# Splitting the long rows of a load into descriptors of at most 7 KB in a DMA-bound im2col kernel

## Chip, cores, metric

The kernel runs on one core of a Trainium2 chip. Times are device microseconds (us) of whole executions, as the device reports them. Durations of single packets are in nanoseconds (ns). An execution that is over 1.5% above the fastest of its kernel counts as slow, the others as fast; ratios compare fast ones alone. A ratio whose 95% interval lies within 2% of 1 gets the verdict "same".

## The reference

The reference unfolds 3x3 patches of a batch of images (im2col). Input: 16 images, 64 channels, 32x32, float32, 4.19 MB. Output: 16 x 576 x 900, 33.18 MB.

```python
for b in range(batch):
    for i in range(h_out):            # 30
        for j in range(w_out):        # 30
            patch = x[b, :, i:i + 3, j:j + 3].copy()
            cols[b, :, col_idx] = patch.ravel()
            col_idx += 1
```

## The kernel before

Each of 128 partitions takes 8 channels (256 image rows of 128 bytes, 32 KB). Three loads bring them in: rows 0 to 32 (4,096 bytes per partition), rows 32 to 200 (21,504 bytes, "the bulk"), rows 200 to 256 (7,168 bytes). VectorE (DVE) and ScalarE (ACT) copy 72 shifted windows into output tiles. Five stores write them out: two of one channel each (32,400 bytes per partition), three of two channels (64,800 bytes). All eight DMAs are issued from SP and share one queue. The first store is made to wait until the bulk load has landed; below that wait is called the gate.

```python
    def load(queue, r0, r1):
        return queue.dma_start(
            out=in_flat[:, r0 * W : r1 * W], in_=x_v[:, r0 * W : r1 * W]
        )

    cuts = [0, H, 200, CPP * H]
    first = load(nc.sync, cuts[0], cuts[1])
    bulk = load(nc.sync, cuts[1], cuts[2])
    load(nc.sync, cuts[2], cuts[3])
    # ... cut: per pair of channels, 18 copies on DVE or ACT ...
            if c == 0:
                st = nc.sync.dma_start(out=out_v[:, s], in_=...)   # cut
                if s == 0:
                    tc.add_manual_dep(st.ins, bulk.ins.name, ...,  # cut
                        reason="the store follows the bulk of the loads")
        if c > 0:
            nc.sync.dma_start(out=out_v[:, c : c + 2]..., in_=out_tile...)  # cut
```

## Time and profile before

| What | Value |
|---|---|
| Time before the prediction, 3 runs | 91.44 us (91.39 to 91.49) |
| Time of the execution that was profiled | 91.84 us |
| DMA packets, bytes | 1152, 37.37 MB |
| DMA packets' share of 16 engines' span | 97.0% |
| DVE and ACT busy | 26% and 29% |

The page's lines are shown in the prediction. Its second section cuts the span in 40 slices. The row "DMA" there is the busy share of the 16 DMA engines in tenths. A DMA engine is not one of the compute engines: each of the 16 takes 8 partitions of every transfer here and works through its packets in order.

### The profile page before, as it was taken

What the parts mean: (1) busy time and instruction counts of PE and PEld (TensorE: products, weight loads), DVE (VectorE), ACT (ScalarE), POOL (GpSimd) and SP (SyncE); (2) the same over time, 40 slices, a digit from 0 to 9 for tenths busy, and PEclk for the clock granted to TensorE, in tenths of its full rate; (3) what the DMA queues carried; (4) which work ended last, traced back from release to release, by engine and by line L of the source; (5) the groups of instructions that cost most, each with busy time, mean ns of one, the idle gap of its engine ahead of it and who ended that gap; (6) DMA issues with size and microseconds to landing.
All of it is one profiled execution on the core that took longest, in us unless ns stands there. A gap on an engine that the chain in (4) does not pass through costs nothing.

```text
span 90.1 us, 140 instructions
## 1 busy us (share of the span) xinstructions
DVE 23.5 (26%) x43; ACT 26.2 (29%) x30; POOL 0.2 (0%) x4
## 2 busy tenths in 40 slices
DVE  0380399970000089600000399300000000000000
ACT  5391399940000089920000399300000000000000
POOL 0000000000000000000000000000000000000000
DMA  5999899999599999993799999999999999947990
GB/s 129 486 382 449 360 518 446 460 460 446 259 460 460 691 460 432 460 432 173 345 460 460 460 460 460 460 460 460 460 460 460 460 432 460 403 201 345 460 460 0
DMA packets 1152, 37.37 MB, mean 415 GB/s; under 512 B 128, under 2 KB 128, under 8 KB 384
## 3 DMA queue, kind: packets, MB, share of 16 engines
q1 hardware_dynamic: 1152, 37.37, 97.0%
HBM read 4.19 MB, written 33.18 MB: 415 GB/s over the span
## 4 chain that ended last, share of the span: by engine, by line
DMA 45%; DVE 16%; DVEq 1%; issue 0%; SPq 0%
DMA out_dram<-out_tile 35%; DVE out_tile L57 16%; DMA in_tile<-in_x_dram 11%; DVEq L93 1%; DVEq L57 0%; SPq L75 0%
## 5 line engine op out<-in xcount | busy, mean ns | idle before, releaser
L55 ACT COPY out_tile<-in_tile 128x900 f32<-128x900 f32 x29 | 24.9, 938 | 30.1 <-DMA out_dram<-out_tile 25.3
L57 DVE COPY out_tile<-in_tile 128x900 f32<-128x900 f32 x43 | 23.5, 624 | 33.6 <-DMA out_dram<-out_tile 26.0
L55 ACT ACT_TABLE_LOAD x1 | 1.3, 1283 | 0.8 <-PEq L122 0.8
L122 POOL MEMSET const-bfloat16-1.0<- 128x1 bf16 x1 | 0.1, 102 | 0.0
L122 POOL MEMSET const-uint8-127<- 128x1 uint8 x1 | 0.1, 102 | 0.0
L122 POOL MEMSET const-float32-0.0<- 128x1 f32 x1 | 0.1, 99 | 0.2 <-issue 0.2
L122 POOL MEMSET const-float32-1.0<- 128x1 f32 x1 | 0.1, 99 | 0.0
## 6 DMA issues: line engine op xcount, KB each, us to landing
out_dram<-out_tile SPq DMA_DIRECT2D x3, 8100.0 KB, 31.3
out_dram<-out_tile SPq DMA_DIRECT2D x2, 4050.0 KB, 14.9
in_tile<-in_x_dram SPq DMA_DIRECT2D x1, 2688.0 KB, 9.6
in_tile<-in_x_dram SPq DMA_DIRECT2D x1, 896.0 KB, 11.4
in_tile<-in_x_dram SPq DMA_DIRECT2D x1, 512.0 KB, 3.6
```

Of the source, the lines that this page charges most:

```text
L55: nc.scalar.copy(out=dst, in_=src)
L57: nc.vector.tensor_copy(out=dst, in_=src)
L93: tc.compile()
L122: nc = _bacc.Bacc("TRN2", target_bir_lowering=False, num_devices=1)
```

## The change

The loads pass a limit of 7,168 bytes for the last dimension of a descriptor. The intent is presumably a smoother stream of reads: pieces of equal size instead of rows of 21 KB.

```diff
     def load(queue, r0, r1):
 
         return queue.dma_start(
-            out=in_flat[:, r0 * W : r1 * W], in_=x_v[:, r0 * W : r1 * W]
+            out=in_flat[:, r0 * W : r1 * W],
+            in_=x_v[:, r0 * W : r1 * W],
+            max_dma_last_dim=7168,
         )
```

Only the bulk exceeds the limit. Each of its rows becomes three descriptors.

## The prediction

> **What bounds the kernel now.** I read the page first: the busy shares of the engines, then its slices and its DMA queue, then the DMA issues, then the queue's own waits, and last the single packet records of the trace. The page of the kernel before:
>
> ```profile
> span 90.1 us, 140 instructions
> ...
> DVE 23.5 (26%) x43; ACT 26.2 (29%) x30; POOL 0.2 (0%) x4
> ...
> DMA  5999899999599999993799999999999999947990
> ...
> DMA packets 1152, 37.37 MB, mean 415 GB/s; under 512 B 128, under 2 KB 128, under 8 KB 384
> ## 3 DMA queue, kind: packets, MB, share of 16 engines
> q1 hardware_dynamic: 1152, 37.37, 97.0%
> ...
> out_dram<-out_tile SPq DMA_DIRECT2D x3, 8100.0 KB, 31.3
> out_dram<-out_tile SPq DMA_DIRECT2D x2, 4050.0 KB, 14.9
> in_tile<-in_x_dram SPq DMA_DIRECT2D x1, 2688.0 KB, 9.6
> in_tile<-in_x_dram SPq DMA_DIRECT2D x1, 896.0 KB, 11.4
> in_tile<-in_x_dram SPq DMA_DIRECT2D x1, 512.0 KB, 3.6
> ```
>
> Both compute engines are idle for over 70% of the span, while the packets of the one DMA queue fill 97.0% of 16 engines' span. The single weaker digits of the DMA row are where slices hold few starts of long packets, not gaps (the packet records below show none). So the bound is the transfer of 37.37 MB, of which 4.19 MB are loads. The five stores are 8100 KB x3 and 4050 KB x2; the change doesn't touch them. Of the three loads, the one of 2688 KB (128 rows of 21,504 bytes) is the "21 KB per partition", the one of 896 KB (rows of 7,168 bytes) the "7 KB".
>
> Then the chain of waits, in order of time, and the queue's waits in the first 25 us:
>
> ```profile
> 0.79 9.62 DMA in_tile<-in_x_dram
> 10.41 0.02 issue
> 10.43 9.24 DVE out_tile L57 x17
> ...
> 19.74 31.24 DMA out_dram<-out_tile
> ```
>
> ```profile
> SPq L60 <- DMA in_tile<-in_x_dram: 8.8, 1, 8.8
> SPq L75 <- DVE out_tile L57: 5.5, 1, 5.5
> ```
>
> The chain seems to say that the bulk load, then 9.24 us of copies, set the end. That is misleading: the store issued at 19.74 lands 31.24 us later because it queues behind the two stores before it. Its first packet starts at 31.11 us, 11.4 us after its issue, so the copies have 11.4 us of slack (the last two stores likewise: the last is issued at 57.2 and starts at 69.40). What does matter is the first line of the queue's waits: the first store may only be issued when the bulk load has landed on all 16 engines, at 10.41 us.
>
> The packet records (start, duration and bytes of each descriptor) can be sorted to 16 engines, because on an engine each packet starts 3 to 4 ns before the end recorded for the previous one. So sorted:
> - From its first packet (1.36 to 1.71 us) to its last (88.5 to 89.13 us) each engine is never idle, except for up to 0.26 us in all in the load stage of a few. There is no gap between the last 7,168-byte packet (ends from 11.89 us on) and the first store packet.
> - Steady step from one packet to the next: 4,096 B in 155.5 ns, 7,168 B in 268 ns, 21,504 B in 795 ns, 64,800 B in 2,387 ns.
> - 15 engines end between 88.52 and 88.79 us. One ends at 89.13 us and sets the end (the span closes about 0.93 us after it; the time of 91.44 us is another 1.4 us longer). That engine lost its time at the start of the bulk load: its first 21,504-byte packets took 1,381 and 1,076 ns in place of 799, after a gap of 136 ns. Its bulk load ran from 3.155 to 10.417 us, 7.26 us against 6.36 to 6.82 us on the others. It is also the one that lands the bulk load at 10.41 us.
>
> **What the Trainium skill says.** "DMA: Bandwidth & Descriptors", section "Where 436 GB/s comes from": 435.2 GB/s is the limit of 16 ports, 27.2 bytes/ns an engine. The trace agrees: 64,800/2,387 is 27.15 bytes/ns, 21,504/795 is 27.05. Its section "Why small descriptors are slow (HBM only)" names a fixed cost of about 3 cycles per packet. Fitting the trace's steps with 27.2 bytes/ns: 268 - 263.5 = 4.5 ns, 795 - 790.6 = 4.4 ns, 155.5 - 150.6 = 4.9 ns. So about 4.5 ns per descriptor, which is of the order that page gives. Section "Why a DMA increments its semaphore by 16 and not by 1": the engine count comes from the slowest dimension, here 128 before and after, so all 16 engines still share the bulk load by partitions, and it counts as landed when the slowest of them is done; the landing at 10.41 us beside 9.74 us for the fastest engine agrees.
>
> **The change part by part.** The comparison of the instruction streams shows one difference: the bulk load's pattern is 128x3x1792 in place of 128x5376. The limit is 7,168, in bytes: 1792 floats. The first load (4,096-byte rows) and the third (exactly 7,168) stay as they are. Order, waits, semaphores, copies and stores are unchanged.
> - Removed: 128 packets of 21,504 B. Added: 384 of 7,168 B. So 256 packets more (1152 to 1408), 16 more on each engine. "Under 8 KB" should go from 384 to 768.
> - Cost in the steady state: a row goes from 795 to 3 x 268 = 804 ns, 9 ns more. Eight rows per engine: 72 ns. Since every engine is busy to the end, those 72 ns lie on the path in full.
> - Issue: a load takes SP 333 to 424 ns to issue. A third dimension may add something to one of them. The bulk is issued at 0.79 us, and its packets are first wanted at 3.0 us, so that is hidden.
> - The gate of the first store moves with the bulk by the same 72 ns, and so do the ends of the 7,168-byte packets: no new gap.
> - Intended gain, as I read it: engines with smaller pieces recover better at the start or stay more even. The most to gain is the lag of the one slow engine, 89.13 - 88.79 = 0.34 us, if it vanished.
> Sum: +0.07 us certain, and between 0 and -0.34 us for the lag. I weigh a partial gain of about 0.11 us: -0.04 us, so 91.40 us.
>
> **Rivals.**
> 1. The lag persists (for: the same addresses are read in the same order, and three executions spread only 91.39 to 91.49, so the lag seems to repeat). Then 91.44 + 0.07 = 91.51 us.
> 2. The lag vanishes, since shorter descriptors hold the engine for a shorter time when the read side is slow. For: the engine's first two bulk packets alone cost 0.58 + 0.28 us over 799. Against: the 4,096-byte packets before them stall as well (up to 984 ns in place of 159), so small packets are no cure. Then 91.44 + 0.07 - 0.34 = 91.17 us.
> 3. The stalls spread: more packets at the start, more engines hit, or another hit harder. Then the slowest ends 0.2 to 0.4 us later, 91.7 to 91.9 us.
> 4. The gate: if the bulk lands later on one engine but the others are through with their 7,168-byte packets, these idle until the store arrives. The first store is issued at 10.50 us and its first packet starts at 11.89 us, 1.39 us later; the very first load took 1.36 us from issue to packet. So the gate is only about 0.03 us from being felt. But the laggard itself has 2.15 us of third load after its bulk, more than 1.36 us, so it never waits; the others would only use up their slack of about 0.34 us against it. Up to that it costs nothing, and beyond it little: under 0.3 us.
> 5. The bulk really comes faster because 21,504-byte packets are inefficient. Against: they run at 27.05 bytes/ns against 27.15 for the largest. There is nothing to win there. If it were so for the whole stage, 1% of 6.4 us is 0.06 us.
>
> **Range and chances.** The outcomes lie between rival 2 (91.17) and rival 3 (91.9), with runs spreading 0.05 us each way and another chip perhaps 0.1. Eight in ten: 91.05 to 91.80 us. Two per cent are 1.83 us: faster by that would need a fifth of the load stage (10.6 us) to vanish while it already runs near the packets' rate; slower by that would need each of 16 new packets per engine to cost 115 ns, where the third load's packets cost 4.5. Hence 1% each, 98% within.
>
> **What would show it right or wrong.** The page should list 1408 packets. In the packet records the bulk pieces should step by 268 ns, and an undisturbed engine's bulk should take about 6.43 us in place of 6.36. The bulk's landing should lie between 9.95 us (lag gone) and 10.5 us (lag kept), and the spread of the engines' ends should show how much of the 0.34 us is left. Stores should be identical, 2,387 ns a packet, with DVE and ACT copies at 624 and 938 ns. Wrong would be: pieces stepping by clearly more than 268 ns, idle time between an engine's third load and its first store packet, or fewer than 16 engines in the bulk.

## The result

| | Median | Range | Runs |
|---|---|---|---|
| Before | 91.50 us | 91.39 to 91.53 | 6 |
| Changed | 91.66 us | 91.61 to 92.06 | 6 |

The ratio is 1.0027, with a 95% interval of 1.0009 to 1.0045; that is 0.08 to 0.41 us. A ratio is the mean time of one kernel's fast runs over the mean of the other's of the same rounds, so it is not quite the ratio of these medians. The change costs a little: 0.16 us by the medians here, and 0.12 us when all executions are pooled (91.55 us over 45 executions of the kernel before, 91.67 us over 12 of the changed one). The pool mixes chips; resampling its executions gives 0.06 to 0.22 us.

The page of the changed kernel (profiled execution: 91.61 us):

```profile
span 89.8 us, 140 instructions
...
DMA  4999999998899999875999999999999997689990
...
DMA packets 1408, 37.37 MB, mean 416 GB/s; under 512 B 128, under 2 KB 128, under 8 KB 768
## 3 DMA queue, kind: packets, MB, share of 16 engines
q1 hardware_dynamic: 1408, 37.37, 97.2%
...
in_tile<-in_x_dram SPq DMA_DIRECT2D x1, 2688.0 KB, 9.3
in_tile<-in_x_dram SPq DMA_DIRECT2D x1, 896.0 KB, 11.0
```

Two things stand out. There are 256 more packets, all under 8 KB, and the stream is still full (97.2%). And the span is *shorter* than in the first profile of before (90.1 us) although the measured times are longer. The chain of waits of the changed kernel has the bulk landing 0.30 us earlier, at 10.11 us in place of 10.41:

```profile
0.80 9.31 DMA in_tile<-in_x_dram
10.11 0.02 issue
10.13 9.24 DVE out_tile L59 x17
```

Read naively, that is a gain of 0.3 us. It is none: the first profile of before was taken on an execution of 91.84 us, that of the changed kernel on one of 91.61 us. So the first thing to test was whether the two profiles may be compared at all.

### The profile page after: what moved, and what is told of

Read it like the earlier page. It is cut to its first block, busy times and chain, and to the rows that moved or that the text cites. A ratio compares the mean times of both kernels' runs of the same rounds, so it can differ in the third digit from the quotient of the medians.

```text
span 89.8 us, 140 instructions
## 1 busy us (share of the span) xinstructions
DVE 23.5 (26%) x43; ACT 26.2 (29%) x30; POOL 0.2 (0%) x4
## 2 busy tenths in 40 slices
DMA packets 1408, 37.37 MB, mean 416 GB/s; under 512 B 128, under 2 KB 128, under 8 KB 768
## 3 DMA queue, kind: packets, MB, share of 16 engines
q1 hardware_dynamic: 1408, 37.37, 97.2%
## 4 chain that ended last, share of the span: by engine, by line
DMA 45%; DVE 16%; DVEq 1%; issue 0%; SPq 0%
DMA out_dram<-out_tile 35%; DVE out_tile L59 16%; DMA in_tile<-in_x_dram 10%; DVEq L95 1%; DVEq L59 0%; SPq L77 0%
```

## How the experiments were read

Every packet of the trace was assigned to a DMA engine as in the prediction. One correction: the prediction put all packet times 0.36 us too late against the instruction clock, because it aligned the end of the last packet of a load with the moment at which its landing was seen. The start of the first load's issue is the right zero. In the first profile of before the first packet starts at 1.01 us (not 1.36), the last engine ends at 88.77 us (not 89.13), and a landing is seen 0.35 us after the last packet's end. All packet times below are on the corrected clock. Differences between packets are not touched.

On that clock one rule holds in all 14 profiles: the time of the profiled execution is the end of the *last* DMA engine plus 3.04 to 3.11 us. "Lag" is how far that last end lies behind the mean of the 16. The prediction measured it from the second-latest engine instead; so measured, the four lags of the table are 0.34, 0.13, 0.05 and 0.19 us.

| Kernel | Profiled execution, us | Mean end of engines, us | Last end, us | Lag, us | Mean of 32,400-byte store packets, ns |
|---|---|---|---|---|---|
| before, first profile | 91.84 | 88.31 | 88.77 | 0.46 | 1,202.3 |
| before, second | 91.57 | 88.20 | 88.46 | 0.26 | 1,201.4 |
| changed, first | 91.61 | 88.30 | 88.52 | 0.22 | 1,205.0 |
| changed, second | 91.93 | 88.37 | 88.85 | 0.48 | 1,204.6 |

The split itself is seen best on engines without a stretched packet. Their eight bulk rows took 6,366 ns in both profiles of before and 6,441 ns in both of the changed kernel: 75 ns more, where the prediction said 72.

## Experiments

Kernels are compared only within the same rounds. The theories: (A) the lag is an accident of single executions, against (B) it belongs to the kernel before and the change removes it. And for the cost: (1) about 4.5 ns for each added descriptor on each engine, (2) a fixed cost of the three-dimensional pattern, (3) about 10 ns for each.

### Both kernels once more

No edit.

> The kernel before, unchanged, for a second profile. The first profile was of an execution of 91.84 us, 0.35 us above the usual 91.39 to 91.53. Theory A (the one slow DMA engine of that profile was an accident of that execution, not the kernel's habit): the new profile, if its own time is below 91.6, shows no engine that ends over 0.3 us after the rest, the bulk load lands at about 10.0 us, span about 89.7. Theory B (the lag belongs to the kernel, and the change removed it): a new profile again shows one engine ending about 0.35 us late, span 90.1. Timing: ratio 1.000 within 0.002.

Measured: 91.62 us median against 91.64 of the kernel before in the same rounds, ratio 0.9986 (0.9939 to 1.0033). The profile, of an execution of 91.57 us:

```profile
span 89.8 us, 140 instructions
...
q1 hardware_dynamic: 1152, 37.37, 97.1%
```

```profile
0.79 9.14 DMA in_tile<-in_x_dram
9.94 0.02 issue
```

The unchanged kernel lands its bulk at 9.94 us here, earlier than the changed one did. Theory A holds, theory B falls. In the bulk and the third load, 12 packets are more than 2.7% longer than usual (the longest 926 ns in place of 799), a third of the 36 in the first profile (longest 1,381).

> The changed kernel, unchanged, in the same call. Theory 1 (about 4.5 ns for each of 16 more descriptors per engine): 0.07 us over the kernel before. If the first measurement's difference of 0.16 us is real and has a second part, 0.13 to 0.19 us again. If it was chip-to-chip or run-to-run noise, it may even be near 0.

Measured: 91.68 us median (91.59 to 91.93) against 91.64, ratio 0.9988 (0.9946 to 1.0031). Runs of before were noisy (91.47 to 92.80, three of eleven above 92.1), so the ratio tells nothing about a tenth of a microsecond. The profile fell on the execution of 91.93 us:

```profile
span 90.1 us, 140 instructions
...
q1 hardware_dynamic: 1408, 37.37, 96.9%
```

```profile
0.78 9.69 DMA in_tile<-in_x_dram
10.47 0.02 issue
```

Now the changed kernel has the laggard: a lag of 0.48 us (0.19 behind the second-latest), and the bulk lands at 10.47 us. So both kernels have executions with a late engine and executions without. Over 91.85 us were 7 of the 45 executions of before and 2 of the 12 of the changed kernel.

### The bulk in 12 pieces

```diff
-            max_dma_last_dim=7168,
+            max_dma_last_dim=7168 if r0 != H else 1792,
```

> Only the bulk load changed further: each row of 21,504 bytes in 12 descriptors of 1,792 instead of 3 of 7,168. That is 88 more per engine than before. Theory 1 (4.5 ns each, on the bound path in full): 0.40 us over the kernel before, packets stepping by about 70 ns. Theory 2 (the cost is fixed, from the third dimension of the pattern or its issue): about 0.16 us, as with 3 pieces. Theory 3 (each descriptor costs about 10 ns, as 0.16 us over 16 would give): 0.88 us.

Measured: 92.46 us (92.35 to 92.50), 0.82 us over the median of before; ratio 1.0067 (1.0026 to 1.0109). By the medians this met theory 3, and not theory 1; the interval of the ratio (0.24 to 1.0 us) leaves room for both, because the runs of before were noisy. The packet records say more. In the first six of the 16 sixteenths of the bulk's packets nearly all took 74 ns (a step of 70 to 71, 4 to 5 ns over 1,792/27.2 = 65.9, theory 1 again). From about 5.7 us on the packets took 79.8 ns on average, scattered between 74 and 86. So there is a descriptor cost of 4 ns, and a second term of about 6 ns that comes and goes. What sets it on was not found.

### The bulk in 24 pieces

```diff
-            max_dma_last_dim=7168,
+            max_dma_last_dim=7168 if r0 != H else 896,
```

> The bulk load's rows in 24 descriptors of 896 bytes: 184 more per engine. Fixed cost of 4.5 ns: steps of 37 to 38 ns, 0.83 us over before. At the mean rate of the run with 12 pieces (9.3 ns each): 1.7 us. If something supplies the 16 engines with one descriptor per 4.7 ns at most (75.8 ns per engine, which is the step in the second half of the bulk with 12 pieces): steps of about 76 ns, the bulk takes 14.5 us, 8 us over before.

Measured: 92.40 us (92.31 to 92.46) against 91.54, so 0.86 us; ratio 1.0088 (1.0053 to 1.0123). Theory 1 said 0.83. The packets are almost all of 41 ns, a step of 37.4 to 37.6 with no second term, and the store packets are at 1,200.3 ns. Twice the pieces of the run above cost the same time, so theory 3 and a limit on the supply of descriptors both fall. So does theory 2: the pattern has the same three dimensions as with 3 pieces, and the cost is not 0.16 us. The page, and what SP issued:

```profile
span 90.6 us, 140 instructions
...
DMA packets 4096, 37.37 MB, mean 413 GB/s; under 512 B 128, under 2 KB 3200, under 8 KB 3456
```

```profile
0.00 6.21 SPq L35 DMA_DIRECT2D in_tile<-in_x_dram  x3
```

The 3,072 pieces of 896 bytes are in the count under 2 KB, and 184 x 4.5 ns = 0.83 us is what they should cost. The third load's issue alone took 4.99 us here, against 0.42 us before and 0.48 us in the changed kernel. It cost nothing: that load's first packet came at 10.06 us, with no gap before it.

### The bulk in 6 pieces, twice

```diff
-            max_dma_last_dim=7168,
+            max_dma_last_dim=7168 if r0 != H else 3584,
```

> The bulk load's rows in 6 descriptors of 3,584 bytes: 40 more per engine than before, against 16 in the change and 88 with 12 pieces. Theory 1 with an added constant (4.5 ns a descriptor, and 0.06 us in the first two stores, whose packets averaged 1,205 ns in place of 1,201.5 in every kernel with a split bulk): 0.18 + 0.06 = 0.24 us over the kernel before. Theory 3 (about 10 ns for each descriptor): 0.40 us. Packets of 3,584 bytes stepping by 136 ns under theory 1.

Measured: 92.12 us median, but from 91.78 to 93.13; ratio 1.0093 (1.0037 to 1.0149). Inconclusive by time: four of six executions were 0.2 to 1.4 us above the profiled one (91.78 us). The step is 136 to 137 ns for most packets, as theory 1 has it.

> The kernel with the bulk in 6 descriptors of 3,584 bytes once more, unchanged, on whatever chip comes. Its first six executions spread from 91.78 to 93.13 us, while its one profile, of the fastest, agreed with theory 1 (mean end of the engines 0.29 us above before). If the spread belongs to the kernel: again several executions above 92.2. If it was that chip or chance: median 91.75 to 91.85 and at most two of six above 92.0. Whatever the time of the profiled execution, it should be the end of the last engine plus 3.09 us, within 0.03.

Measured: 91.82 us (91.73 to 91.96) against 91.60, so 0.22 us, ratio 1.0016 (0.9992 to 1.0040). That fits theory 1 with its added constant (0.24), though the interval (-0.07 to 0.37 us) holds no difference too. The bulk took about 6.62 us per engine, where 4.5 ns a descriptor make 6.55, so a little of the second term seen with 12 pieces is here too. The wide spread didn't come back. Its profiled execution took 91.85 us and its last engine ended 3.09 us before that, as foretold. Why the first six spread so was not found.

### The bulk in 2 pieces

```diff
-            max_dma_last_dim=7168,
+            max_dma_last_dim=10752,
```

> The bulk load's rows in 2 descriptors of 10,752 bytes: 8 more per engine. Theory 1 (4.5 ns each): 0.04 us over the kernel before, plus at most 0.06 us in the first two stores if their slower packets come with any split of the bulk (1,205 ns in place of 1,201.5). Packets stepping by 400 ns. If ten ns each: 0.08 us. All of that is near what the rounds can tell; the steps in the trace decide.

Measured: the fast runs are at ratio 0.9997 (0.9956 to 1.0039); no difference of 0.04 us can be seen in that. The step is 400 ns, as expected. Three of six executions were over 93 us and the profile fell on one of them (93.96 us), so it is not compared with the others. None of the 11 executions of before was slow; whether this split brings slow ones was not tested again. The profile is still a clean picture of what one late engine does here: one packet took 1,434 ns, the last engine ended the bulk at 11.90 us while the fifteen others had ended it by 9.74 us, the gate opened late (first store issued at 12.32 us), and no engine had a store packet before 13.16 us.

### The stores split, the loads not

Loads as before; the stores' rows in pieces of 6,480 and 7,200 bytes.

```diff
                     in_=out_tile[:, s].rearrange("p kk i j -> p (kk i j)"),
+                    max_dma_last_dim=7200,
...
                 in_=out_tile.rearrange("p c kk i j -> p (c kk i j)"),
+                max_dma_last_dim=7200,
```

> Loads as before, but the stores split: rows of 32,400 bytes in 5 pieces of 6,480, rows of 64,800 in 9 pieces of 7,200. 16 x 4 + 24 x 8 = 256 more descriptors per engine. Theory 1 carried over to stores: 256 x 4.5 = 1.15 us over the kernel before (ratio 1.0126). If the 4.5 ns belong to loads alone: 0. If 10 ns each: 2.6 us.

Measured: 94.31 us (94.22 to 94.77), 2.67 us over 91.64; ratio 1.0282 (1.0236 to 1.0327). Divided by 256 that is 10.4 ns a descriptor: a miss for theory 1 as carried over to stores.

```profile
DMA packets 5248, 37.37 MB, mean 402 GB/s; under 512 B 128, under 2 KB 128, under 8 KB 5120
## 3 DMA queue, kind: packets, MB, share of 16 engines
q1 hardware_dynamic: 5248, 37.37, 97.8%
```

The queue is *fuller* than before (97.8% against 97.0%), and slower. The share counts the time that packets take, not the bytes they carry: the GB/s beside it (402 against 415) are what fell. The 7,200-byte packets step by 275 ns on average against 264.7 at 27.2 bytes/ns, the 6,480-byte ones by 249 against 238.2. So a store descriptor costs about 10 ns on average where a load descriptor of 7,168 bytes costs 4.5. (The profile fell on the slowest execution, 94.77 us.)

The average hides two parts. But for a handful, the shortest steps of 7,200-byte packets are 269 to 270 ns, about 5 ns over, like a load's; the rest varies from packet to packet. The unsplit stores have both parts too: in the second profile of before their 64,800-byte packets step by 2,387 ns at their most frequent, 4.6 ns over 64,800/27.2, and by 2,392.4 ns on average, 10 ns over. Pieces of 7,200 and 6,480 bytes are not multiples of 256, and the Trainium skill ("DMA: Bandwidth & Descriptors", section "How a descriptor splits into AXI transactions") says that a descriptor that doesn't start on a 256-byte boundary spends extra beats. The trace speaks against that as the cause. By it, the cost would depend on a piece's place in its row, as each place of a 7,200-byte piece starts 32 bytes further past a boundary, and the ninth on one again. But all nine places have steps of 270 ns or less, and no place is cheapest in all three stores. What makes the varying part, about 5 ns here as with 12 pieces, stays open.

### Three DMAs instead of one pattern with three pieces

```diff
-    cuts = [0, H, 200, CPP * H]
+    cuts = [0, H, 88, 144, 200, CPP * H]
     first = load(nc.sync, cuts[0], cuts[1])
-    bulk = load(nc.sync, cuts[1], cuts[2])
-    load(nc.sync, cuts[2], cuts[3])
+    load(nc.sync, cuts[1], cuts[2])
+    load(nc.sync, cuts[2], cuts[3])
+    bulk = load(nc.sync, cuts[3], cuts[4])
+    load(nc.sync, cuts[4], cuts[5])
```

> The bulk load as three DMAs of 56 image rows each, 7,168 bytes per partition, two-dimensional patterns; the first store waits for the third. The same 24 data descriptors of 7,168 bytes per engine as in the change, two more semaphore packets, but in piece order, not in row order. If the change's cost comes from the number of descriptors: 0.07 to 0.16 us over the kernel before, as the change, plus about 0.02 for the semaphore packets. If it comes from the three-dimensional pattern: the bulk's steps stay 268 ns but the first two stores return to 1,201.5 ns and the total is 0.07 to 0.1 us. Copies of the second channel should start about 4 us earlier, with no gain in time, since the DMA queue is the bound.

Measured: 91.64 us median (91.59 to 92.30) against 91.54, so 0.10 us; ratio 1.0022 (0.9982 to 1.0063). With the same number of descriptors and no third dimension the median is that of the change. The interval (-0.16 to 0.58 us) can't settle theory 2 alone; the step can help: undisturbed it is 268 ns, with the third dimension as without. The profile fell on the slowest execution (92.30 us, lag 0.76 us), so its other means aren't used. Its chain shows what the early pieces brought:

```profile
3.55 11.99 DVE out_tile L59 x22
15.54 0.02 issue
```

The copies run without a break from 3.55 us and the third store is ready at 15.54 us in place of 19.7, and the time is no better for it. Compute is not the bound.

### The gate: taken away, and moved later

The changed kernel without the gate (each store still waits for its own copies):

```diff
-                if s == 0:
+                if False:
                     tc.add_manual_dep(st.ins, bulk.ins.name, ...
```

> The changed kernel without the wait of the first store for the bulk load (the store still waits for its own copies, so no race). The first store is then issued at about 7.1 us in place of 10.2. If the gate costs time at the hand-over from loads to stores: faster than the changed kernel by up to 0.1 us. If there is no idle time there, as the packet records show: the same as the changed kernel within 0.05 us, ratio to the kernel before 1.001 to 1.002. If descriptor generation for the stores disturbs the last packets of the third load (they rose from 272 to 273 to 285 ns once the first store was issued), that disturbance moves to 8 us.

Measured: 92.90 us (92.67 to 93.05) against 91.54, ratio 1.0140 (1.0103 to 1.0177). That is a miss: a gain of up to 0.1 us or no change was expected, and the store's early issue costs 1.2 us over the changed kernel (91.67 us, from other calls). What SP issued, from the timeline (start, length, first to last of the group):

```profile
0.00 1.70 SPq L35 DMA_DIRECT2D in_tile<-in_x_dram  x3
7.06 6.77 SPq L62 DMA_DIRECT2D out_dram<-out_tile  x2
```

```profile
in_tile<-in_x_dram SPq DMA_DIRECT2D x1, 2688.0 KB, 9.3
in_tile<-in_x_dram SPq DMA_DIRECT2D x1, 896.0 KB, 12.2
```

The bulk still lands 9.3 us after its issue, as with the gate. The third load, which is in the queue ahead of the store, takes 12.2 us in place of 11.0. From about 9 us on load packets of 7,168 bytes stretch from 272 to as much as 829 ns (the next expectation says 680), and no store packet starts before 12.67 us. The load packets of one engine add up to 10.03 us on average against 8.73 with the gate: 1.31 us more. The stores give back 0.13 us. That the early issue of the store slows the loads ahead of it is shown; how is not.

The kernel before without the gate (the same edit):

> The kernel before without the wait of the first store for the bulk load. The changed kernel without it took about 1.3 us more, its last load packets stretched to as much as 680 ns while the store's descriptors were queued behind them. If that belongs to the early store and not to the split: 1.1 to 1.5 us over the kernel before here too, with the 7,168-byte packets well above 272 ns. If only split loads are disturbed: within 0.1 us of the kernel before.

Measured: fast runs at ratio 1.0134 (1.0089 to 1.0180), so about 1.2 us. The cost belongs to the early store, not to the split.

The gate on the third load instead of the bulk, in the kernel before:

```diff
-    load(nc.sync, cuts[2], cuts[3])
+    last = load(nc.sync, cuts[2], cuts[3])
...
-                        bulk.ins.name,
+                        last.ins.name,
```

> The kernel before with the first store waiting for the third load instead of the bulk. Landing 0.35 us after the last packet's end, 0.09 us to the issue, 1.0 us to the first store packet: every engine idles between loads and stores, the last one 1.4 to 1.5 us. So 1.3 to 1.5 us over the kernel before, with store packets at 1,200 ns since all engines start together, and a spread of the engines' ends below 0.2 us.

Measured: 93.18 us median of four (92.88 to 93.73), ratio 1.0171 (1.0130 to 1.0211), unclear at 2%. The best execution and the profiled one (92.97 us) lie 1.3 to 1.4 us over 91.60; the mean difference, 1.6 us, is a little above the expected 1.3 to 1.5.

```profile
12.19 1.50 SPq L60 DMA_DIRECT2D out_dram<-out_tile  x2
```

The first store is issued at 12.19 us, its first packets start at 13.04 us, and the ends of the engines differ by 0.19 us. One expectation failed: the store packets are at 1,207.6 ns on average although all engines start together, not at 1,200. The gate on the bulk lies between two errors that cost over a microsecond each, and the change moves it too little to matter.

No experiment pointed to a version that beats both kernels: splits in three or more pieces cost time, and the one in two showed no gain. Fewer descriptors, with the bulk and the third load in one, were not tried.

## Why the prediction was right, and which step of it failed

- **The number.** The measured 91.66 us lies inside the stated range of 91.05 to 91.80 us. But the best guess, 91.40 us, was a gain of 0.04 us, and the change cost 0.12 to 0.16 us. The range was wide because of the lag, which the change doesn't govern, so that the result fell into it says little about the mechanism.
- **The bound** was right. In every profile the time follows the last DMA engine.
- **The cost of the split**, 72 ns, was right in its parts: 1408 packets, a step of 268 ns for 7,168 bytes, 75 ns measured on undisturbed engines, and about 4.5 ns a descriptor down to 896 bytes (184 more: 0.86 us measured, 0.83 worked out). With 12 pieces, and in small with 6, a second term came on top. The issue grew as foreseen, from 333 to 388 ns for the bulk, and stayed hidden.
- **The gain term failed**: "I weigh a partial gain of about 0.11 us" of a lag of 0.34 us. It took one profile of one engine for a property of the kernel ("the lag seems to repeat"). The warning was in the data: the profiled execution took 91.84 us while the three timed ones lay between 91.39 and 91.49, and the excess of 0.40 us was about the lag. Its sum "the time of 91.44 us is another 1.4 us longer" set the span of that execution against the time of others; against its own time the difference is 1.8 us, as in every profile. The second profiles swap the roles, lag 0.26 us for before and 0.48 us for the changed kernel. Nothing to win was found; the term should have been 0.
- **A term was missing**: the first two stores. Their 16 packets per engine averaged 1,205.0 and 1,204.6 ns in the two profiles of the changed kernel, 1,202.3 and 1,201.4 in those of before. That is 2.95 ns x 16 = 0.05 us. Together with 0.07 it makes 0.12 us, the pooled difference; that the two agree so closely is partly luck, since the pool is good to 0.1 us at best. This second part was seen, not explained, and that the split causes it is not shown. It does not follow the number of descriptors: with 24 pieces these packets were at 1,200.3 ns, in the changed kernel without the gate at 1,200.2, and with the unsplit loads and a late gate at 1,207.6.
- **Rival 1** (91.51 us) had the right mechanism, minus the missing 0.05 us; most of the rest of its distance to 91.66 is that before stood at 91.50 with these rounds counted. Rivals 2 and 3 were stories about the lag. Rival 4 was right that the late engine never waits at the gate itself; with the bulk in 2 pieces it had no gap while the other fifteen idled 1.1 to 1.8 us. Rival 5 was right that nothing was to win in the rate.
- The 0.36 us error of the packet clock changed no term, since only differences entered. The margin at the gate stands: in the first profile 1.04 us from issue to first store packet against 1.01 us for the first load.

What stays open: the 0.05 us in the stores, the varying term of about 5 ns that packets of 12 pieces and of stores show, the cause of the lags, and why a store that is issued early slows loads.

## What to carry to other kernels

When the DMA queue is full from end to end, count descriptors per engine: each one more costs its few nanoseconds on the path, so don't split rows that already run near the rate of the largest packets. Before an effect is read off one profile, compare that execution's own time with the other executions; if it is off by the effect, take a second profile. An order between loads and stores in one queue can be worth ten times more than the sizes of their pieces.

## What the Trainium skill lacked or had wrong

- "DMA: Bandwidth & Descriptors", section "Why small descriptors are slow (HBM only)", gives a cost of about 3 cycles per packet, and no measured time for it. Here load descriptors from 896 to 21,504 bytes each cost 4 to 5 ns over 27.2 bytes/ns; without that rate, 24 x 37.5 - 795 = 105 ns for 23 more descriptors is 4.6 ns each. No page that I found has the varying part: stores in pieces of 6,480 and 7,200 bytes cost about 10 ns each on average.
- The same page, section "Latency and other measured facts", has about 0.6 us to the first byte for this path, and doesn't say from where it counts. The profiles show 1.00 to 1.02 us from the start of the first load's issue to its first packet, and 0.62 to 0.64 us from that issue's end; the second agrees.
- No page of it that I read says that a store issued early behind loads in the same queue slows those loads: 7,168-byte packets went from 272 to as much as 829 ns, 1.2 us in all.
- The same section on latency calls two of the engines usually slower and, as a best guess, ties that to the other, software descriptor path. Here, on the hardware path, one of 16 engines ended 0.46 to 0.48 us behind the mean in one profile of each kernel, and 0.22 to 0.26 us in the other; the records don't name the engine.
